# A matrix product with scaled sum on one Trainium2 core: one weight load for two products, a last store behind the joined section, and one load of addends in two pieces

## The chip, the cores and the metric

The kernel runs on one core of one Trainium2 chip. The core has a matrix engine (TensorE, PE in the profile, with its weight loads as PEld), a vector engine (VectorE, DVE), a scalar engine (ScalarE, ACT), a general engine (GpSimd, POOL), and SyncE (SP), which here only waits on semaphores and issues transfers (DMAs) between the chip's memory (HBM) and the core's. The metric is the device time of one execution in microseconds.

## The reference

```
batch, m, k, n = 16, 512, 1024, 768
x: (16, 512, 1024) float32, weight: (1024, 768) float32, scale = 0.1, add_value: (16, 512, 768) float32
return (scale * np.matmul(x, weight) + add_value).astype(np.float32)
```

So 8192 rows of x, each of 1024 values, are multiplied by one 1024 x 768 matrix, scaled, and added to 8192 rows of 768 addends. Inputs read and output written are 87.03 MB together.

## The kernel before, in words

The rows are cut into 64 tiles of 128 rows; tiles go in groups of 8, of which a partition holds 8 neighbouring rows, so that a transfer of 8 tiles moves long pieces. Everything is in one section with semaphores written out by hand (`tile_critical`, L205 to L210). In it each engine has its own program.

**SyncE** (`sync_engine`, L84) walks the list STREAM (L19) in order: ("x", s, n) loads n tiles of x from tile s on, "w" a half of the weights, "a" the addends, "o" stores results. Ahead of each issue it waits for what that transfer needs. Loads of x (L105) wait until the slots of `xs` (16 tiles) were read by the casts (L101, L102). Loads of addends (L115) wait for all loads of addends before them (L109), and from tile 32 on for the store that empties their slots of `ao` (32 tiles, L113, L114); addends of 48-55 therefore wait for the store of 16-23. Stores (L123) wait until the store two before has landed (L121) and until the results are made (L122). As all issues are on one engine, a wait also holds back all that stands behind it in the list. The list ends with loads of x 56-59 and 60-63, addends 56-63, and the stores of 32-39, 40-47, 48-55 and 56-63. Then SyncE waits until the last two stores have landed (L127, L128).

**ScalarE and GpSimd** (`mover`, L130) cast x to bfloat16, 4 tiles (a move) at a time, into one of two buffers `va`; each does 8 of the 16 casts of a move (L143). Each waits for the load of x and for the buffer to be free.

**VectorE** (`vector_engine`, L146) casts the weights at the start (L151). Then, for each pair of tiles, it transposes one pair of x from `va` to `xt` (`turn`, L158, which waits for both casting engines where a move begins) and finishes another pair: `finish` (L163, L167) takes the products from `mm`, scales them, adds the addends in `ao` and leaves the result there. The order is written out by hand in `group` (L171): wait for the addends of the group of 8, then four times finish a pair and turn a pair that lies four tiles further on. The first two turns of a group take the second half of a move whose first half was turned already; the third and fourth turn take the next move. The wait for addends (L172) stands ahead of all of these, the turns too.

**TensorE** (`tensor_engine`, L187) goes over the tiles, in a loop with 4 of them in its body. Ahead of each pair of tiles it waits for the turn and for the finish that frees the products' space (`mm`, 4 tiles). For each of the 8 pieces of 128 values of k it makes two products, of 512 and of 256 columns of the weights (CUT, L198), each a matmul with the piece of x as its stationary operand (L199). Each matmul becomes a weight load and a product, 1024 of each.

Of the kernel before, what the change touches and what calls it, by code (L numbers as in the profile page):

```python
# [7 lines left out]
P = 128  # L8
G = 8
X_SLOTS = 16  # L10
A_SLOTS = 32
CUT = 512
# [13 lines left out]
]  # L26


@with_exitstack
def kernel(  # L30
# [8 lines left out]
    nc = tc.nc  # L39
# [7 lines left out]
    _, N = weight.shape  # L47
    T = M // P
    KC = K // (2 * P)
    KJ = 2 * KC  # L50
# [3 lines left out]
    out_v = out_f.rearrange("(g p t) n -> p g t n", p=P, t=G)  # L54
    w_v = weight.rearrange("(c p r) n -> p c (r n)", p=P, r=2)

    def rows(view, s, n):
        assert s // G == (s + n - 1) // G
        return view[:, s // G, s % G:s % G + n, :]
# [5 lines left out]
    ao = const.tile([P, A_SLOTS, N], fp32, name="ao")  # L65
    w_bf = const.tile([P, KJ, N], bf16, name="w_bf")
    va = [const.tile([P, MOVE * KC, 4, 64], bf16, name=f"va{i}") for i in range(VA_BUFS)]
    xt = const.tile([P, XT_TILES, KC, P], fp32, name="xt")
    mm = psum.tile([P, MM_BUFS, 1024], fp32, name="mm")

    w_sem = [tc.alloc_semaphore(f"w{i}") for i in range(2)]
    x_sem = [tc.alloc_semaphore(f"x{i}") for i in range(X_SLOTS // MOVE)]
    a_sem = tc.alloc_semaphore("a")
    o_sem = [tc.alloc_semaphore(f"o{i}") for i in range(2)]
    by_act, by_pool, pool_go, turned, casts, done, made = (
        tc.alloc_semaphore(name)
# [4 lines left out]
    def slot(t):  # L81
        return (t + G) % A_SLOTS

    def sync_engine(eng):  # L84
        loads, stores, known = [], [], {}

        def need(sem, value):
            if known.get(sem, 0) < value:
                eng.wait_ge(sem, value)  # L89
                known[sem] = value  # L90

        for op, s, n in STREAM:
            last = s + n - 1
            if op == "w":
                dst = ao[:, s:s + n, :].rearrange("p (c r) n -> p c (r n)", r=2)
                move, sem = eng.dma_start(dst, w_v[:, s // 2:(s + n) // 2, :]), w_sem[s // 4]
            elif op == "x":
                k = s % X_SLOTS
                if last >= X_SLOTS:
                    moved = 8 * (last + 1 - X_SLOTS) // MOVE  # L100
                    need(by_act, moved)  # L101
                    need(by_pool, moved)  # L102
                    if n == 2 * MOVE:
                        eng.sem_inc(x_sem[k // MOVE + 1], 16)
                move = eng.dma_start(xs[:, k:k + n, :], rows(x_v, s, n))  # L105
                sem = x_sem[k // MOVE]
            elif op == "a":
                if loads:
                    need(a_sem, 16 * len(loads))  # L109
                if slot(s) == 0:  # L110
                    need(casts, KJ)
                if s >= A_SLOTS:
                    i = stores.index((s - A_SLOTS, n))  # L113
                    need(o_sem[i % 2], 16 * (i // 2 + 1))  # L114
                move = eng.dma_start(ao[:, slot(s):slot(s) + n, :], rows(add_v, s, n))  # L115
                sem = a_sem
                loads.append((s, n))
            else:
                i = len(stores)
                if i > 1:  # L120
                    need(o_sem[i % 2], 16 * (i // 2))  # L121
                need(made, MADE + last + 1)  # L122
                move = eng.dma_start(rows(out_v, s, n), ao[:, slot(s):slot(s) + n, :])  # L123
                sem = o_sem[i % 2]
                stores.append((s, n))
            move.then_inc(sem, 16)
        for i in (len(stores) - 2, len(stores) - 1):  # L127
            need(o_sem[i % 2], 16 * (i // 2 + 1))  # L128

    def mover(eng, copy, parity, count, go=None):  # L130
        if go is None:
            eng.preload_act_table(mybir.ActivationFunctionType.Copy)  # L132
        with eng.Fori(16, 16 * (T // X_SLOTS) + 1, 16) as i:
            for q in range(X_SLOTS // MOVE):
                eng.wait_ge(x_sem[q], i)
                eng.wait_ge(turned, i + (4 * q - 12) if q < 3 else i)  # L136
                if go is not None:
                    eng.sem_inc(go, 1)
                k = MOVE * q
                src = xs[:, k:k + MOVE, :].rearrange("p i (c b k) -> p (i c) b k", b=4, k=64)  # L140
                for a in (parity, parity + 2):
                    for b in range(4):
                        copy(va[q % VA_BUFS][32 * b:32 * b + 32, :, a, :],  # L143
                             src[32 * a:32 * a + 32, :, b, :]).then_inc(count, 1)

    def vector_engine(eng):  # L146
        ao_g = ao.rearrange("p (g t) n -> p g t n", t=G)

        def cast_w(s, n):
            eng.wait_ge(w_sem[s // 4], 16)  # L150
            eng.tensor_copy(w_bf[:, s:s + n, :], ao[:, s:s + n, :]).then_inc(casts, n)  # L151

        def turn(move, half, moves=None):
            if half == 0:
                eng.wait_ge(by_act, moves)
                eng.wait_ge(by_pool, moves)  # L156
            q = 2 * half * KC
            eng.transpose(  # L158
                xt[:, 2 * half:2 * half + 2, :, :].rearrange("p i c m -> p (i c m)"),
                va[move % VA_BUFS][:, q:q + 2 * KC, :, :].bitcast(fp32).rearrange("p c a k -> p (c a k)"),  # L160
            ).then_inc(turned, 2)

        def finish(pair, at, products):  # L163
            eng.wait_ge(done, products)  # L164
            a = ao_g[:, at, 2 * pair:2 * pair + 2, :]
            q = 2 * (pair % 2)
            eng.scalar_tensor_tensor(  # L167
                a, mm[:, q:q + 2, 0:N], float(scale), a,
                op0=mybir.AluOpType.mult, op1=mybir.AluOpType.add).then_inc(made, 2)

        def group(i, at, last):  # L171
            eng.wait_ge(a_sem, i)  # L172
            for p in range(4):
                finish(p, at, i + (4 * p - 12) if p < 3 else i)
                if p < 2 or not last:
                    turn(1 if p < 2 else 0, p % 2, i + 8 if p == 2 else i)

        cast_w(0, 4)
        cast_w(4, 4)
        turn(0, 0, 8)  # L180
        turn(0, 1)
        with eng.Fori(16, 2 * T, 16) as i:
            group(i, bass.ds((i // 16) % (A_SLOTS // G), 1), False)
        s = slot(T - G) // G
        group(2 * T, slice(s, s + 1), True)

    def tensor_engine(eng):  # L187
        eng.sem_inc(turned, TURNED)
        eng.sem_inc(made, MADE)
        eng.wait_ge(casts, KJ)  # L190
        with eng.Fori(TURNED + 2, TURNED + 2 + T, XT_TILES) as i:
            for q in range(XT_TILES):
                if q % 2 == 0:
                    eng.wait_ge(turned, i + q if q else i)
                    eng.wait_ge(made, i + q if q else i)
                for j in range(KJ):
                    x2 = xt[:, q, j // 2, :].bitcast(bf16).rearrange("p (m r) -> p r m", r=2)
                    for n0, n1 in ((0, CUT), (CUT, N)):  # L198
                        m = eng.matmul(  # L199
                            mm[:, q, n0:n1], x2[:, j % 2, :], w_bf[:, j, n0:n1],  # L200
                            start=(j == 0), stop=(j == KJ - 1))
                if q % 2:
                    m.then_inc(done, 4)

    with tc.tile_critical(no_gpsimd_drain=True):  # L205
        sync_engine(nc.sync)
        mover(nc.scalar, nc.scalar.copy, 0, by_act)
        mover(nc.gpsimd, nc.gpsimd.tensor_copy, 1, by_pool, pool_go)
        vector_engine(nc.vector)
        tensor_engine(nc.tensor)  # L210


# [33 lines left out]
```

## Time and profile before

| What | Value |
|---|---|
| Median of 3 runs | 211.11 us (210.85 to 211.26) |
| The profiled execution's own time | 210.75 us |
| Its span, first to last instruction | 208.7 us |
| Bytes moved, mean rate over the span | 87.03 MB, 417 GB/s |
| DMA engines' time in packets, share of the span | 97.7% |
| PE busy | 171.2 us (82%), 1024 matmuls |
| PEld busy | 101.5 us (49%), 1024 weight loads of 99 ns |
| DVE busy | 98.0 us (47%) |
| ACT and POOL busy | 134.7 us (65%) and 135.4 us (65%) |
| Mean granted clock of PE | 0.974 |

The profile is of one execution. A line of instructions gives the start and the length in us, the engine, the line of the kernel, the operation, what it writes and reads with the shape, the number of instructions merged into it, and in brackets how long the engine had been idle and who released it. A table by stretches gives for each stretch of the span the busy time of each engine with its instructions, the granted clock (1.00 is full speed), the share of the DMA engines and GB/s. "Busy tenths" cut the span in 40 slices of 5.2 us, one digit each.

### The profile page before, as it was taken

The page shows a single profiled execution, that of the slowest core. Times are in us where ns is not written, and L with a number is a line of the kernel's source. Part 1 is how long each engine was busy: PE and PEld are TensorE (multiplying, and loading weights), DVE is VectorE, ACT ScalarE, POOL GpSimd, SP SyncE. Part 2 cuts the span into 40 slices and gives each one's busy share as a digit, 9 for nine tenths or more (in the row PEclk, how much of TensorE's full clock was granted, in tenths as well). Part 3 has the DMA queues.
Part 4 walks back from the last instruction along what each step waited for, and adds up shares of the span by engine and source line. Part 5 has one row for each costly group of instructions (what it writes and reads, how often), then busy time and mean ns, then how long its engine had stood idle before and what let it go on. Part 6 is the DMA issues. An engine that isn't in the chain of part 4 may idle for free.

```text
span 208.7 us, 2743 instructions
## 1 busy us (share of the span) xinstructions
PE 171.2 (82%) x1024; PEld 101.5 (49%) x1024; DVE 98.0 (47%) x66; ACT 134.7 (65%) x129; POOL 135.4 (65%) x132
## 2 busy tenths in 40 slices
PE   0000899999999999999999999999996699999600
PEld 0000455566556666666666666655663366665300
DVE  0045325555555555555555555555522825555300
ACT  2392966995499999988780799459960399900000
POOL 0398966996499999999680799559970299900000
PEclk9999999999999999999999999999999799999975
DMA  6999999999999999999999999999999999999785
GB/s 210 419 435 437 433 427 430 446 449 433 402 427 477 399 411 477 396 452 419 415 438 411 454 424 429 452 422 433 419 429 429 424 451 415 443 438 429 339 382 226
DMA packets 4576, 87.03 MB, mean 417 GB/s; under 512 B 480, under 2 KB 480, under 8 KB 992
## 3 DMA queue, kind: packets, MB, share of 16 engines
q1 hardware_dynamic: 4576, 87.03, 97.7%
HBM read 61.87 MB, written 25.17 MB: 417 GB/s over the span
## 4 chain that ended last, share of the span: by engine, by line
DMA 45%; PE 40%; POOL 5%; DVE 3%; issue 1%; SPq 0%; DVEq 0%; POOLq 0%
PE mm L199 40%; DMA out_dram<-ao 27%; DMA ao<-in_add_value_dram 14%; POOL va L143 5%; DMA xs<-in_x_dram 4%; DVE ao L167 2%; DVE xt L158 1%; DVEq L167 0%; SPq L105 0%; SPq L115 0%; DVEq L164 0%; DVEq L156 0%; POOLq L136 0%; SPq L89 0%; SPq L241 0%
## 5 line engine op out<-in xcount | busy, mean ns | idle before, releaser
L199 PE MATMUL mm<-w_bf,xt 128*128 128x512 bf16 (+1 forms) x1024 | 171.2, 331 | 25.4 <-DVE xt L158 25.4
L143 POOL CAST va<-xs 32x1024 bf16<-32x1024 f32 x128 | 135.2, 1056 | 47.2 <-DMA xs<-in_x_dram 31.4
L143 ACT CAST va<-xs 32x1024 bf16<-32x1024 f32 x128 | 133.5, 1043 | 46.7 <-DMA xs<-in_x_dram 40.9
L199 PEld LDWEIGHTS mm<-w_bf,xt 128*128 128x128 bf16 x1024 | 101.5, 99 | 94.8 <-DVE xt L158 25.8
L167 DVE SCALAR_TENSOR_TENSOR ao<-mm,ao 128x1536 f32 (+1 forms) x32 | 56.2, 1757 | 81.1 <-PE mm L199 72.9
L158 DVE STREAM_TRANSPOSE xt<-va 128x1024 f32<-128x1024 f32 x32 | 39.5, 1235 | 5.8 <-POOL va L143 5.7
L151 DVE CAST w_bf<-ao 128x3072 bf16<-128x3072 f32 x2 | 4.5, 2265 | 13.6 <-DMA ao<-in_weight_dram 13.6
L132 ACT ACT_TABLE_LOAD x1 | 1.3, 1283 | 0.9 <-SPq L205 0.9
L227 POOL MEMSET const-float32-0.0<- 128x1 f32 x1 | 0.1, 98 | 0.2 <-issue 0.2
L227 POOL MEMSET const-bfloat16-1.0<- 128x1 bf16 x1 | 0.1, 100 | 0.0
L227 POOL MEMSET const-float32-1.0<- 128x1 f32 x1 | 0.1, 98 | 0.0
L227 POOL MEMSET const-uint8-127<- 128x1 uint8 x1 | 0.1, 98 | 0.0
## 6 DMA issues: line engine op xcount, KB each, us to landing
ao<-in_add_value_dram SPq DMA_DIRECT2D x8, 3072.0 KB, 17.0
out_dram<-ao SPq DMA_DIRECT2D x8, 3072.0 KB, 27.2
xs<-in_x_dram SPq DMA_DIRECT2D x8, 2048.0 KB, 21.3
xs<-in_x_dram SPq DMA_DIRECT2D x4, 4096.0 KB, 23.1
ao<-in_weight_dram SPq DMA_DIRECT2D x2, 1536.0 KB, 12.3
```

The costliest lines, as they stand in the source:

```text
L132: eng.preload_act_table(mybir.ActivationFunctionType.Copy)
L143: copy(va[q % VA_BUFS][32 * b:32 * b + 32, :, a, :], src[32 * a:32 * a + 32, :, b, :]).then_inc(count, 1)
L151: eng.tensor_copy(w_bf[:, s:s + n, :], ao[:, s:s + n, :]).then_inc(casts, n)
L158: eng.transpose(xt[:, 2 * half:2 * half + 2, :, :].rearrange("p i c m -> p (i c m)"), va[move % VA_BUFS][:, q:q + 2 * KC, :, :].bitcast(fp ...
L167: eng.scalar_tensor_tensor(a, mm[:, q:q + 2, 0:N], float(scale), a, op0=mybir.AluOpType.mult, op1=mybir.AluOpType.add).then_inc(made, 2)
L199: m = eng.matmul(mm[:, q, n0:n1], x2[:, j % 2, :], w_bf[:, j, n0:n1], start=(j == 0), stop=(j == KJ - 1))
L227: nc = _bacc.Bacc("TRN2", target_bir_lowering=False, num_devices=1)
```

## The change

It has three parts.

First, the matmul is replaced by `product`: it issues the weight load by itself, once for each piece of x, and then the two products of 512 and 256 columns, marked as bringing no load of their own.

Second, the addends of 48-55 are loaded as 48-51 and 52-55. The second piece reports to a semaphore of its own, `a_late`, which does not take part in the order of the other loads of addends. TensorE raises `a_late` at the start by as much as the first six groups ask for; VectorE waits for it ahead of the third finish of every group but the last.

Third, the store of 56-63 leaves STREAM and is issued after the section in which the engines are synchronised by hand, so that its place and its completion are set by the framework: the section's end joins all engines, and then the store is issued. The waits of SyncE for the last two stores go.

```diff
-    ("x", 44, 4), ("a", 40, 8), ("x", 48, 8), ("o", 16, 8), ("o", 24, 8), ("a", 48, 8),
+    ("x", 44, 4), ("a", 40, 8), ("x", 48, 8), ("o", 16, 8), ("o", 24, 8), ("a", 48, 4), ("a", 52, 4),
     ("x", 56, 4), ("x", 60, 4), ("a", 56, 8), ("o", 32, 8), ("o", 40, 8), ("o", 48, 8),
-    ("o", 56, 8),
 ]
+LAST = (56, 8)
...
-                if loads:
+                if loads and s % G == 0:
                     need(a_sem, 16 * len(loads))
...
-                    i = stores.index((s - A_SLOTS, n))
+                    i = next(j for j, (a, b) in enumerate(stores) if a <= s - A_SLOTS < a + b)
...
-                sem = a_sem
-                loads.append((s, n))
+                if s % G:
+                    sem = a_late
+                else:
+                    sem = a_sem
+                    loads.append((s, n))
...
-        for i in (len(stores) - 2, len(stores) - 1):
-            need(o_sem[i % 2], 16 * (i // 2 + 1))
...
             for p in range(4):
+                if p == 2 and not last:
+                    eng.wait_ge(a_late, i)
                 finish(p, at, i + (4 * p - 12) if p < 3 else i)
...
+    def product(eng, acc, x_j, w_j, j):
+        eng.ldweights(x_j, tile_position=(0, 0))
+        for n0, n1 in ((0, CUT), (CUT, N)):
+            m = eng.add_instruction(mybir.InstMatmult(
+                start_tensor_calc=(j == 0), stop_tensor_calc=(j == KJ - 1),
+                tile_size=(P, P), tile_position=(0, 0), ldweights=False,
+                name=nc.get_next_instruction_name(), engine=eng.engine,
+                ins=[eng.lower_ap(w_j[:, n0:n1]), eng.lower_ap(x_j, for_matmul_weights=True)],
+                outs=[eng.lower_ap(acc[:, n0:n1])]))
+        return m
...
+        eng.sem_inc(a_late, 16 * (T // G - 2))
...
-                    for n0, n1 in ((0, CUT), (CUT, N)):
-                        m = eng.matmul(
-                            mm[:, q, n0:n1], x2[:, j % 2, :], w_bf[:, j, n0:n1],
-                            start=(j == 0), stop=(j == KJ - 1))
+                    m = product(eng, mm[:, q, :], x2[:, j % 2, :], w_bf[:, j, :], j)
...
+    s, n = LAST
+    nc.sync.dma_start(rows(out_v, s, n), ao[:, slot(s):slot(s) + n, :])
```

More of the change, by code (lines that the diff above doesn't have):

```diff
@@ L72 @@
     x_sem = [tc.alloc_semaphore(f"x{i}") for i in range(X_SLOTS // MOVE)]
-    a_sem = tc.alloc_semaphore("a")
+    a_sem, a_late = (tc.alloc_semaphore(n) for n in ("a", "a_late"))
     o_sem = [tc.alloc_semaphore(f"o{i}") for i in range(2)]
```

## The prediction, made before the changed kernel was run

> **What bounds the kernel now.** I read the page's busy tenths first, then the timeline of TensorE (PE), VectorE (DVE) and GpSimd (POOL) around the one dip, then stretches cut at the changes of the granted clock, then the end.
>
> ```profile
> PE   0000899999999999999999999999996699999600
> PEclk9999999999999999999999999999999799999975
> DMA  6999999999999999999999999999999999999785
> ```
>
> The DMA row is full from the second slice to slice 37: 87.03 MB at 417 GB/s over the span, so bytes are the bound and earlier compute there moves no byte. Only the last three slices have DMA room (7, 8, 5), and what decides there is when the last products are ready. PE is busy all along too, except for one dip (6, 6) at 157 to 167 us with a lower clock beside it.
>
> ```profile
> 149.82 9.91 PE L199 MATMUL mm<-w_bf,xt 128*128 128x512 bf16 x60
> 163.59 33.05 PE L199 MATMUL mm<-w_bf,xt 128*128 128x512 bf16 x192 [3.86 <-DVE xt L158]
> ...
> 151.15 1.24 DVE L158 STREAM_TRANSPOSE xt<-va 128x1024 f32<-128x1024 f32 x1
> 160.62 1.76 DVE L167 SCALAR_TENSOR_TENSOR ao<-mm,ao 128x1536 f32 x1 [8.23 <-DMA ao<-in_add_value_dram]
> 162.30 1.24 DVE L158 STREAM_TRANSPOSE xt<-va 128x1024 f32<-128x1024 f32 x1
> ...
> 174.25 1.25 DVE L158 STREAM_TRANSPOSE xt<-va 128x1024 f32<-128x1024 f32 x1 [1.70 <-POOL va L143]
> ...
> 165.42 17.45 POOL L143 CAST va<-xs 32x1024 bf16<-32x1024 f32 x16 [9.94 <-DMA xs<-in_x_dram]
> ```
>
> Here DVE waits 8.23 us for the addends of 48-55, the transposes queued behind that wait are late, and PE stands still for 3.86 us with 192 of 1024 matmuls (tiles 52 to 63) to go. Then the second gate: tiles 56-59 can't be multiplied before POOL has cast their x (it begins when x lands, 165.42) and DVE has turned it (174.25, having waited for POOL).
>
> ```profile
> 160.42:163.83 3.41, 0.24 (x2) 0.12 (x3) 1.00 0.99 423
> 163.83:167.25 3.42, 3.42 (x13) 1.68 (x12) 0.50 1.02 436
> 167.25:170.66 3.41, 3.41 (x22) 2.03 (x21) 1.00 1.07 459
> ...
> 194.55:197.97 3.42, 2.10 (x14) 1.06 (x11) 1.00 0.80 345
> ...
> 20.47:23.89 3.42, 2.34 (x8) 1.03 (x9) 1.00 1.05 453
> ```
>
> The columns are PE busy, weight loads busy, granted clock, DMA share, GB/s. After 3.41 us with 0.24 us of PE work the clock fell to 0.50, and 13 matmuls fit where 22 did; after a full stretch it came back. A stretch with 2.10 us of work (61%) did not lower it; one at the start with 2.34 us (69%) did not yet raise it, since the next stretch is also slow (13 matmuls).
>
> The end, in the same columns with all engines (PE, loads, DVE, ACT, POOL):
>
> ```profile
> 184.00:196.00 12.00, 12.00 (x75) 7.23 (x74) 4.91 (x4) 0.00 (x0) 0.00 (x0) 1.00 1.01 436
> ...
> 197.00:198.00 1.00, 0.00 (x0) 0.00 (x0) 1.00 (x1) 0.00 (x0) 0.00 (x0) 1.00 0.07 25
> 198.00:199.00 1.00, 0.00 (x0) 0.00 (x0) 0.51 (x1) 0.00 (x0) 0.00 (x0) 1.00 0.06 25
> 199.00:200.00 1.00, 0.00 (x0) 0.00 (x0) 0.00 (x0) 0.00 (x0) 0.00 (x0) 1.00 0.92 393
> ```
>
> PE ends at 196.66, DVE's last finish runs from 196.75 to 198.51, the last store is issued at 198.59; the DMA engines have run dry from 197 to 199.4. So the path that sets the end is: x of 56-59 lands, cast, turn, 64 pairs of matmuls, finish, last store (8.7 us to landing), exit.
>
> **Part 1, one weight load for two products.** It drops 512 of 1024 loads of 99 ns. The matmuls remain. DVE's last finishes begin at 181.18, 186.35, 191.55 and 196.75, each released by PE: 5.2 us for two tiles, which is 16 pairs (512 and 256 columns), so 325 ns a pair. In the trace the starts of the matmuls lie alternately 216 ns (after 512 columns) and 109 ns (after 256) apart: twice the columns, twice the time, and what is fixed per matmul is 2 x 109 - 216 = 2 ns. Each of these matmuls has its own load of 98 ns in front, so the loads run beside the products, and nearly nothing of them is in the pace. A load dropped per pair gains at most 2 ns, 0.13 us over the last 64 pairs; the other bound is that the load that is left is no longer done ahead: a loss of 98 ns x 64 = 6.3 us there. Value taken: 0, by the row of 109 ns, in which even the shorter product covers a load; now two products cover one.
> [...]
>
> **Part 2, addends of 48-55 in two loads.** One more issue on SP (0.33 us, row of L115), ahead of the two x issues; the DMA engines have the store of 24-31 before them then, so this costs 0. By the chain, that load was issued at 145.44, when the store of 16-23 had landed, and landed at 160.29: 14.85 us for that store of 24-31 and itself, 3.1 MB each, 7.4 us each. Its first half then lands 3.7 us earlier, at 156.6. DVE needs 3.3 us from landing to PE's restart (160.29 to 163.59): restart at 159.9, where PE ran out at 159.73. So the 3.86 us stall shrinks to 0.2. The second half lands when the whole did, 160.3; its new wait stands ahead of the third finish, which waits for PE until about 165.4 anyway: 0.
> Next late thing: tiles 52-55 are 4 x 2.6 = 10.4 us, now warm, so PE is done at 170.3 (record 170.5). Tile 56 waits for a transpose that still ends at 174.25 + 1.25 = 175.50, since x is behind the same bytes in a full queue, and POOL's cast begins when it lands. PE restarts at 175.55. Before, PE reached tile 56 at 196.66 - 20.8 - 0.16 (the last record outlasts its 109 ns of pace by 0.16) = 175.70. The gain is 0.15 us; **the stall is moved, not removed**: 5.0 us of idle directly ahead of the last 64 pairs.
> Price of that: before, the cold stretch (3.4 us at half clock, 1.7 us lost) was absorbed by the wait for x. Now it is on the path. If the stretches lie as in this profile (next ends at 170.66, 174.07, 177.49, 180.90), 170.66 to 174.07 is empty, the clock falls at 174.07; 174.07 to 177.49 holds 1.94 us of work (57%, below the 69% that did not raise it), so it rises at 180.90: 5.35 us at half clock, **2.68 us lost**. If they lie otherwise: a cold time between 2.4 us (just enough work to raise it at once) and 6.8 us (two stretches), a loss of 1.2 to 3.4 us.
> [...]
>
> **Part 3, last store behind the joined section.** Off the path: the exit's join. Now the last landing is at 207.27, SP's join (L205) runs from 207.48 to 207.79, the closing part (L241) to 208.69: 1.42 us. The store's landing is then followed by the closing part alone, about 0.9: -0.52. On the path: DVE's end to issue was 0.08 us; the join's answers between the engines take 0.31, so about 0.3: +0.22 (bounds 0 and 0.5). Moved past on SP: the two waits for stores 48-55 and 56-63 go, and the wait for 40-47 ahead of the issue, which had landed by 192.5; no other issue is behind it.
>
> **Sum**, against the profiled execution (span 208.7, time 210.75): -0.15 + 2.68 + 0.22 - 0.52 = +2.23 us, 213.0. The runs' median is 211.11, 0.36 above that execution: 213.3. With the middle of the losses from 1.2 to 3.4 us, 2.3, it is 213.0. I take **213.2**, nearer to the first, since its positions were seen.
>
> **Rivals.**
> (a) The gap stays warm. If the 5.0 us of idle is split by a stretch's end so that neither part counts as idle, nothing is lost: -0.15 + 0.22 - 0.52 = -0.45, 210.7 (210.5 to 210.9 by the join's bounds): not slower. It decides where idle fills too little of each stretch: 7% of work lowered the clock, 61% did not, the point is between. If only up to 0.24 us of work lowers it, 5.05 + 0.24 - 3.41 = 1.9 us of the 3.41 us of possible positions do so ahead of the restart and another 0.24 behind it, 62% of them; if up to 2.10 us does, all do. For it: only that. Against it: in this profile's positions an entire stretch is empty. Chance 0.18.
> (b) The split does not do what it says: both halves land together because the queue mixes them. Then the stall and the cold stretch stay where they were, and only part 3 counts: -0.3, 210.8. Against it: the load and the x behind it landed one after the other (160.3, 165.4). Chance 0.06.
> (c) The remaining loads become visible, say because a load can't be done ahead while two products share the weights: up to 98 ns x 512 = 50 us of PE, and with PE's start at 21.5, its 171 us of work and the 12 us from its end to the span's, some 255. Against it: part 1. Chance 0.04.
> The forecast, a cold restart on the path, gets 0.72, with its own range 211.9 (loss 1.2) to 214.1 (loss 3.4).
>
> **Numbers.** A measurement of this kernel tells about 0.2% (0.4 us) from no change. Faster by more: half of (a) and a third of (b), 0.11. Within: the rest of these, 0.13. Slower: forecast and (c), 0.76. The likeliest has less than 8 in 10, so the range takes in (a) and (b): 210.5 to 214.2.
>
> **What would show it.** Right: PE's gap at 159.7 gone or under 0.5 us; a gap of some 5 us that ends at 175.5, released by a transpose that waited for POOL; granted clock 0.50 after it; about 22 to 24 us from there to PE's end; the last store issued at some 201 us; under 1 us from its landing to the span's end; matmuls still 325 ns a pair with 512 loads. Wrong: clock 1.00 after the gap (then (a)); the gap still at 160 (then (b)); a pace above 325 ns (then (c)) or below 323 (then part 1 was undervalued); x of 56-59 landing before 163 us.

## The result, and the profile after

The changed kernel takes 212.65 us (median of 10 runs, 211.70 to 213.01), the kernel before 211.10 us (10 runs, 210.82 to 211.88). The ratio is 1.0066, with a 95% interval of 1.0047 to 1.0084: slower by 1.0 to 1.8 us. The profiled execution took 212.22 us, with a span of 210.2 us where the one before had 208.7.

The page's busy tenths of the changed kernel, the same three rows as of before:

```profile
PE   0000999999999999999999999999998946999700
PEclk9999999999999999999999999999999995999985
DMA  6999999999999999999999999999999999999577
```

The dip of PE has moved by two slices to the right, so it now ends where the last eight tiles begin, and the low clock stands behind it. The dip of the DMA row at the end is deeper (5 instead of 7 in the third slice from the end).

The timelines of PE, DVE and POOL around it (start and length in us; a few matmul records are missing from this trace, so counts and single idle times are a little off):

```profile
148.79 10.24 PE L193 MATMUL mm<-w_bf,xt 128*128 128x512 bf16 x61
159.83 10.57 PE L193 MATMUL mm<-w_bf,xt 128*128 128x512 bf16 x63 [0.81 <-DVE xt L159]
175.47 22.98 PE L193 MATMUL mm<-w_bf,xt 128*128 128x512 bf16 x126 [5.07 <-DVE xt L159]
...
156.86 1.76 DVE L168 SCALAR_TENSOR_TENSOR ao<-mm,ao 128x1536 f32 x1 [5.18 <-DMA ao<-in_add_value_dram]
...
174.17 1.25 DVE L159 STREAM_TRANSPOSE xt<-va 128x1024 f32<-128x1024 f32 x1 [7.06 <-POOL va L144]
...
165.34 17.45 POOL L144 CAST va<-xs 32x1024 bf16<-32x1024 f32 x16 [9.90 <-DMA xs<-in_x_dram]
```

The stall at 160 us has nearly gone: DVE's wait for the addends is 5.18 us instead of 8.23, and PE's idle time 0.81 us by its row instead of 3.86, of which some 0.3 us is a pair of products missing from the trace. But x of 56-59 lands when it did (POOL begins at 165.34, before at 165.42), the transpose comes when it did (174.17, before 174.25), and PE, done with tiles 52-55 at 170.41, stands still for 5.07 us until 175.47. From there to PE's end are 22.98 us; before, the same 64 pairs took 21.0.

Stretches cut at the changes of the clock (PE busy, weight loads, DVE, ACT, POOL, then granted clock, DMA share, GB/s):

```profile
169.34:172.75 3.41, 1.07 (x7) 0.20 (x2) 0.00 (x0) 3.31 (x5) 3.23 (x4) 1.00 1.01 432
172.75:176.17 3.42, 0.70 (x3) 0.26 (x2) 2.00 (x2) 3.35 (x4) 3.24 (x4) 0.50 1.07 460
176.17:179.58 3.41, 3.41 (x12) 0.76 (x5) 2.04 (x2) 3.34 (x4) 3.17 (x5) 0.50 1.00 432
179.58:182.99 3.41, 3.41 (x22) 1.06 (x11) 0.00 (x1) 2.62 (x3) 3.09 (x3) 1.00 0.94 404
```

The stretches are not chosen freely: the granted clock changed at 27.30, 163.83, 167.25 and 201.38 us in the profile before and at 25.98, 172.75, 179.58 and 203.47 us here, and these changes lie whole multiples of 3.41 us apart (before 136.53, 3.41 and 34.13 us, that is 40, 1 and 10 of them; here 146.77, 6.83 and 23.89 us, that is 43, 2 and 7). The half clock in the tables of three experiments below (6.83, 6.83 and 3.42 us) fits this.

The clock falls at 172.75 inside the gap and is back only at 179.58. So PE worked 4.11 us (175.47 to 179.58) at half clock and lost half of it, 2.05 us, right ahead of the end.

The end: first stretches with the same columns, then, from SP's timeline, the last store's issue:

```profile
198.00:199.00 1.00, 0.45 (x4) 0.00 (x0) 0.44 (x1) 0.00 (x0) 0.00 (x0) 1.00 0.06 25
199.00:200.00 1.00, 0.00 (x0) 0.00 (x0) 1.00 (x1) 0.00 (x0) 0.00 (x0) 1.00 0.00 0
200.00:201.00 1.00, 0.00 (x0) 0.00 (x0) 0.32 (x1) 0.00 (x0) 0.00 (x0) 1.00 0.00 0
201.00:202.00 1.00, 0.00 (x0) 0.00 (x0) 0.00 (x0) 0.00 (x0) 0.00 (x0) 1.00 0.92 393
```

```profile
200.60 0.33 SPq L224 DMA_DIRECT2D out_dram<-ao  x1
```

The DMA engines wait until 201 us, before until 199. The store is issued 0.28 us behind DVE's end at 200.32 (before 0.08), lands 8.7 us later at 209.3, and the span ends 0.9 us behind that (before 1.4).

### The profile page after: what moved, and what is told of

Its sections match the earlier page's. It is cut to its first block, busy times and chain, and to the rows that moved or that the text cites. A ratio compares the mean times of both kernels' runs of the same rounds, so it can differ in the third digit from the quotient of the medians.

```text
span 210.2 us, 2215 instructions
## 1 busy us (share of the span) xinstructions
PE 170.3 (81%) x1008; PEld 50.8 (24%) x512; DVE 97.9 (47%) x66; ACT 134.7 (64%) x129; POOL 135.4 (64%) x132
## 4 chain that ended last, share of the span: by engine, by line
DMA 63%; POOL 15%; PE 11%; issue 2%; SPq 2%; DVE 1%; POOLq 0%; DVEq 0%
DMA xs<-in_x_dram 29%; DMA out_dram<-ao 27%; POOL va L144 15%; PE mm L193 11%; DMA ao<-in_add_value_dram 7%; DVE ao L168 1%; SPq L115 1%; DVE xt L159 1%; SPq L105 1%; SPq L96 0%; POOLq L137 0%; SPq L104 0%; POOLq L139 0%; SPq L89 0%; DVEq L157 0%
## 5 line engine op out<-in xcount | busy, mean ns | idle before, releaser
L193 PE MATMUL mm<-w_bf,xt 128*128 128x256 bf16 (+1 forms) x1008 | 170.3, 330 | 28.1 <-DVE xt L159 27.3
L191 PEld LDWEIGHTS <-xt 128*128 128x128 bf16 x512 | 50.8, 99 | 147.2 <-issue 118.3
```

The source lines that it names most:

```text
L191: eng.ldweights(x_j, tile_position=(0, 0))
L193: m = eng.add_instruction(mybir.InstMatmult(start_tensor_calc=(j == 0), stop_tensor_calc=(j == KJ - 1), tile_size=(P, P), tile_position=(0 ...
```

## The experiments

The theory: the split moves PE's stall to the place ahead of the last 64 pairs, where the half clock that follows is on the path. The rivals: the weight loads, the store behind the join, or the split by another way than the clock.

**Part 1 alone** (the kernel before with `product` of the diff, nothing else).

> The kernel before with part 1 alone (512 weight loads instead of 1024). Theory (loads run beside the products): a pair of products stays at 325 ns, the stall of 3.9 us at 160 stays, time as before, 211.1 within 0.2 us. [...]

Measured 211.13 us, ratio 0.9997 (0.9978 to 1.0016). From its table of groups, first the products, then the loads:

```profile
L190 PE MATMUL mm<-w_bf,xt 128*128 128x256 bf16 (+1 forms) x1008 | 170.4, 330 | 26.9 <-DVE xt L158 26.0
...
L188 PEld LDWEIGHTS <-xt 128*128 128x128 bf16 x512 | 50.8, 99 | 146.0 <-issue 118.6 <-DVE xt L158 27.3
```

Half of the loads' 101.5 us is gone and PE's busy time is what it was (171.2 before; 16 records are missing). The loads were beside the products. In this profile the half clock at the old stall lasted 6.8 us, twice as long as in the one of before (PE's timeline, then the stretches):

```profile
163.44 33.90 PE L190 MATMUL mm<-w_bf,xt 128*128 128x512 bf16 x189 [4.50 <-DVE xt L158]
...
158.37:161.79 3.42, 0.57 (x4) 0.07 (x1) 1.32 (x1) 0.00 (x0) 0.00 (x0) 1.00 1.03 438
161.79:165.20 3.41, 1.76 (x6) 0.48 (x4) 3.41 (x4) 0.08 (x1) 0.00 (x0) 0.50 1.00 428
165.20:168.62 3.42, 3.42 (x13) 0.83 (x6) 0.97 (x1) 3.35 (x4) 3.19 (x4) 0.50 1.06 453
```

PE ended at 197.34 here instead of 196.65, with the same program for everything else. The weight loads are not the reason: the profile of part 3 alone (below), with all 1024 loads, has 6.8 us of half clock at the old stall too, and PE ends at 197.12 (33.60 us from its restart, 33.05 in the profile before). So where the stretches fall is a matter of the execution, and a longer time at half clock delays PE's end even at the old place.

**Part 2 alone.**

```diff
-    ("x", 44, 4), ("a", 40, 8), ("x", 48, 8), ("o", 16, 8), ("o", 24, 8), ("a", 48, 8),
+    ("x", 44, 4), ("a", 40, 8), ("x", 48, 8), ("o", 16, 8), ("o", 24, 8), ("a", 48, 4), ("a", 52, 4),
```

with `a_late` as in the diff, and parts 1 and 3 undone.

> The kernel before with part 2 alone (addends of 48-55 in two loads). Theory (the stall moves from 160 to 170-175 and the clock falls ahead of the last 64 pairs): 0.2 us gained at the restart and 1.2 to 3.4 us lost at half clock, 2.0 as in the changed kernel's profile, so 212.1 to 214.1, some 212.9. Rival (the loss of the changed kernel comes from the store behind the join): 210.9 to 211.1.

Measured 213.04 us, ratio 1.0087 (1.0061 to 1.0113). The whole loss comes with this part. PE's timeline in its profile has the same gap, and the stretches by clock show two slow ones behind it:

```profile
159.95 10.58 PE L205 MATMUL mm<-w_bf,xt 128*128 128x512 bf16 x63 [1.08 <-DVE xt L161]
175.61 23.78 PE L205 MATMUL mm<-w_bf,xt 128*128 128x512 bf16 x126 [5.09 <-DVE xt L161]
```

```profile
171.11:174.52 3.41, 0.00 (x0) 0.00 (x0) 0.21 (x1) 3.34 (x4) 3.23 (x4) 1.00 1.01 432
174.52:177.94 3.42, 2.33 (x8) 1.05 (x9) 3.42 (x3) 3.35 (x4) 3.24 (x4) 0.50 1.07 460
177.94:181.35 3.41, 3.41 (x13) 1.67 (x12) 0.41 (x1) 3.31 (x5) 3.23 (x4) 0.50 0.97 418
```

From 175.61 to 181.35 are 5.74 us at half clock, 2.87 lost; the 64 pairs took 23.78 us.

**Part 3 alone** (last store behind the section, its waits gone, the rest as before).

> The kernel before with part 3 alone (last store behind the joined section). Theory: issue 0.2 us later behind DVE's end, exit 0.55 us shorter behind the landing, together -0.3, 210.8. Rival (the join costs what the changed kernel lost): 212 or more.

Measured 210.72 us, ratio 0.9987 (0.9968 to 1.0006). The join does not cost what the change lost; that it gains is likely by this and not shown, since the interval reaches past 1.

**The changed kernel with the gap filled.** Its tile loop is cut ahead of tile 56, and between the two loops stands (FILL is 44, late is the count that tile 56 waits for)

```diff
+        eng.wait_ge(made, late)
+        x_j = w_bf[:, 0, 0:P]
+        for k in range(FILL):
+            if k == 0:
+                eng.ldweights(x_j, tile_position=(0, 0))
+            eng.add_instruction(mybir.InstMatmult(
+                start_tensor_calc=True, stop_tensor_calc=True,
...
+                ins=[eng.lower_ap(w_bf[:, 0, 0:256]), eng.lower_ap(x_j, for_matmul_weights=True)],
+                outs=[eng.lower_ap(mm[:, 0, N:N + 256])]))
```

> The changed kernel with 44 matmuls of 256 columns added in PE's gap ahead of tile 56 (109 ns each, 4.8 us of 5.1), which write to columns of the products' space that nothing reads; the output is as before. Theory (the clock fell because of the gap): granted clock 1.00 up to PE's end at 196.3, time 0.4 us under the kernel before, 210.7. Rival (the split delays the end by something other than the clock, such as the order on DVE): 212.2 to 213 as the changed kernel.

Measured 210.12 us (210.03 to 210.47), ratio 0.9957 (0.9942 to 0.9972). PE's timeline, then stretches over the gap and behind it:

```profile
170.17 4.97 PE L227 MATMUL mm<-w_bf 128*128 128x256 bf16 x44
175.65 20.75 PE L194 MATMUL mm<-w_bf,xt 128*128 128x256 bf16 x124 [0.51 <-DVE xt L160]
```

```profile
170.41:175.65 5.24, 4.73 (x45) 0.10 (x1) 1.53 (x2) 5.12 (x6) 4.94 (x6) 1.00 0.95 408
175.65:179.06 3.41, 3.41 (x22) 1.07 (x11) 2.50 (x2) 3.31 (x5) 3.23 (x4) 1.00 0.99 425
```

PE waits for the same transpose and starts at the same time (the second row begins with a product of 256 columns, so the record of the 512 columns ahead of it, 0.2 us, is missing), the clock stays at 1.00, the 64 pairs take 21.0 us with that record (20.75 without it), and useless work has made the kernel 2.5 us faster than the changed one. With the clock kept up, nothing of the loss is left. It is also 1.0 us faster than the kernel before, not 0.4 as expected. The sum of the other terms (restart, issue, exit) is about -0.5 us, and the executions of the kernel before with the highest granted clock (0.973 to 0.975) took 210.5 to 211.0, so the remaining 0.5 us fits a kernel before that loses time to the clock in many of its executions too.

**Half of that filling** (22 matmuls instead of 44).

> As e4_warm with 22 added matmuls instead of 44: 2.4 us of work at the start of PE's gap, so that some 2.7 us of idle is left, less than one 3.41 us stretch. Theory (a stretch with little enough work lowers the clock, it need not be empty: in the changed kernel's profile one with 1.07 us of work, 31%, did): a stretch over the idle holds at least 0.7 us of work, 21%, so by position some runs fall to half clock and some do not, single runs spread between 210.1 and 213, median 210.5 to 212. Rival (only an empty stretch lowers the clock): always 1.00, 210.1 as e4_warm.

Measured 210.42 us (median, a little under the range expected), ratio 0.9971 (0.9947 to 0.9995). Of 12 executions 8 took 210.12 to 210.56 us and 4 took 211.80 to 212.12. Only one was profiled, and it is of the latter (PE's timeline, then the stretches):

```profile
175.68 22.66 PE L194 MATMUL mm<-w_bf,xt 128*128 128x512 bf16 x128 [2.68 <-DVE xt L160]
```

```profile
173.38:176.79 3.41, 1.11 (x7) 0.39 (x4) 2.42 (x2) 3.34 (x4) 3.23 (x4) 1.00 0.94 404
176.79:180.21 3.42, 3.42 (x13) 0.79 (x6) 1.62 (x2) 3.35 (x4) 3.24 (x4) 0.50 1.00 431
```

A gap of 2.68 us is shorter than a stretch and still lowered the clock, after a stretch with 1.11 us of work (33%). The rival, that only an empty stretch does so, falls.

**x of 56-59 between the two halves of the addends** (the changed kernel, and in the list)

```diff
-    ("x", 44, 4), ("a", 40, 8), ("x", 48, 8), ("o", 16, 8), ("o", 24, 8), ("a", 48, 4), ("a", 52, 4),
-    ("x", 56, 4), ("x", 60, 4), ("a", 56, 8), ("o", 32, 8), ("o", 40, 8), ("o", 48, 8),
+    ("x", 44, 4), ("a", 40, 8), ("x", 48, 8), ("o", 16, 8), ("o", 24, 8), ("a", 48, 4), ("x", 56, 4),
+    ("a", 52, 4), ("x", 60, 4), ("a", 56, 8), ("o", 32, 8), ("o", 40, 8), ("o", 48, 8),
```

> The changed kernel with the load of x 56-59 put between the two halves of the addends of 48-55 in the list. Theory: x 56-59 lands at some 161.5 instead of 165.1, its cast and turn end near 172, PE's gap shrinks from 5.1 to some 1.3 us, the clock stays at 1.00, PE ends 4 us earlier than in e4_warm, near 192.7. The last store is then issued near 195, while the DMA engines still work. Gain over e4_warm, if all 16 DMA queues are dry from 197.4 to 199.4 there: 2 us, 208.1. Rival (one of the queues is behind, as the last landing of the store of 48-55 came 1.3 to 1.6 us behind the 15 others in both profiles, and sets the end however early the store is issued): 0.4 to 0.8 us, 209.3 to 209.7. If the stretch of idle still lowers the clock: 1 to 2 us slower than either.

Measured 209.96 us (209.65 to 210.07), ratio 0.9927 (0.9905 to 0.9949): the fastest kernel of this study. Timelines of PE and SP, then two stretches at the end:

```profile
172.02 20.98 PE L193 MATMUL mm<-w_bf,xt 128*128 128x512 bf16 x128 [1.39 <-DVE xt L159]
...
195.14 0.33 SPq L224 DMA_DIRECT2D out_dram<-ao  x1
```

```profile
198.00:199.00 1.00, 0.00 (x0) 0.00 (x0) 0.00 (x0) 0.00 (x0) 0.00 (x0) 0.50 0.91 393
...
205.60:206.60 1.00, 0.00 (x0) 0.00 (x0) 0.00 (x0) 0.00 (x0) 0.00 (x0) 0.50 0.06 25
```

PE's gap is 1.39 us, PE ends at 192.99, and the last store is issued 5.5 us earlier than in the changed kernel, while the queues work: there is no dry time at 198. Yet this gains little over the filled gap: 0.16 us by the medians, 0.14 by the last landings of the two profiles (207.21 and 207.07). The two kernels were measured on different chips, on which the kernel before took 211.10 and 211.32 us, so the medians say no more than some tenths; the ratios to it, 0.9957 and 0.9927, would say 0.6 us. The last line shows what holds the end: from 205.6 to 206.6 us the DMA share is 0.06, one engine of sixteen. In this store 15 parts landed by 205.59 and one at 207.07, as the store of 48-55 did at 198.35 and 199.81. From the one store to the next are 7.24 us for the 15 parts and 7.26 us for the late one, so the late one had no pause either, and issuing the store earlier could not help it. That it is the same engine both times is inferred from this; the trace doesn't tell which engine a part is of. The rival for the end is right: all of the 2 us was not to be had. Its price of 0.4 to 0.8 us is above what the medians and the landings show, and not excluded by the ratios.

**The last kernel without part 1, and without part 3.**

> As e6_x_between with part 1 undone (1024 weight loads again). No clock loss blurs this one. Theory (loads run beside the products): same as e6_x_between, 209.95 within 0.2 us, PE's last 64 pairs still 21.0 us. [...]

Measured 210.10 us (209.94 to 210.22). PE's last 64 pairs took 20.98 us again, with 1024 loads:

```profile
172.00 20.98 PE L203 MATMUL mm<-w_bf,xt 128*128 128x512 bf16 x126 [1.40 <-DVE xt L159]
```

By this row the loads cost nothing here either. The time is within the 0.2 us expected of 209.96, but says little, since it is of a third chip, on which the kernel before took 210.71 us instead of 211.32.

> As e6_x_between with part 3 undone (last store in the list again, waits for the last two stores at the end). The store is issued while the queues work, so its issue is off the path. Theory: only the exit differs, 1.4 instead of 0.9 us behind the last landing, 0.5 us slower than e6_x_between, 210.5. Rival (the framework's exit costs the same either way): 209.95.

Measured 210.23 us (210.13 to 210.45), beside the 210.10 of the kernel without part 1 on the same chip, and the 209.96 on another. In the profiles the span ends 1.4 us behind the last landing here, and 0.9 us in the kernel with part 3, as expected; in the time only 0.13 of that 0.5 is seen on the same chip (0.27 against the other). The profiled execution of this kernel was the slowest of its 12. The last landing was some 0.15 us earlier here (206.93 beside 207.07 and 207.14). Whether that belongs to the change or to the late part is open.

## Why the prediction was right, and where it was off

What is right is the mechanism, shown by the rows above and by the filled gap. That the time lies in the range says less: 210.5 to 214.2 us would have taken in rivals (a) and (b) as well.

- **Part 1 at nothing**: right. A pair takes 325 ns with 512 loads (four finishes of the profile after start 5.2 us apart), and neither adding it alone nor undoing it in the last kernel changed PE's pace.
- **The stall is moved, not removed**: right. Expected: restart of tile 52 at 159.9, PE idle from 170.3 to 175.55. Measured: 159.83, 170.41 to 175.47.
- **The cold restart on the path**: right in kind. The term was mis-sized: 2.68 us came from the old profile's positions; this profile had 2.05, that of the split alone 2.87. The positions were not the same again (the clock first rose at 27.30 us before, at 25.98 after, at 24.33 with the split alone, with 22, 22 and 23 matmuls in the stretch behind that, and 13 in the stretch ahead of it before and after; the first matmul came at 21.4 to 21.6 in all three), so a draw between 1.2 and 3.4 us is the better picture, and both lie in it.
- **The step that did not hold**: "before, the cold stretch (3.4 us at half clock, 1.7 us lost) was absorbed by the wait for x". That was so in the one execution that was profiled. The wait absorbs about that much and no more. In the profiles of part 1 alone and of part 3 alone the time at half clock at the old place was 6.8 us, and PE ended 0.7 and 0.5 us later. The runs of the kernel before order by their mean granted clock: of the 29 beside the first four experiments, those at 0.973 to 0.975 took 210.5 to 211.0 us, those at 0.967 to 0.968 took 211.1 to 211.5 (one 211.9), those at 0.960 to 0.961 took 211.7 to 211.8. Later runs of it on other chips follow this with exceptions (211.2 and 211.3 us at 0.972, 211.1 at 0.974), and the mean clock also counts the half clock behind PE's end, so this is a sign and no proof. By it the 0.36 us between its profiled execution and its median, which I added as a constant, was most likely itself the price of the clock at the old stall, which the changed kernel no longer has. Without it the sum is 212.6 (loss 2.3) to 213.0 (loss 2.68), against a measured 212.65; with it the forecast of +2.1 us was too large against a measured +1.55.
- **Part 3**: +0.22 on the path, measured 0.28 - 0.08 = 0.20; -0.52 at the exit, measured 0.9 instead of 1.4. With the terms as measured, the sum is -0.23 (restart) + 2.05 + 0.20 - 0.5 = +1.5 us, which is the difference of the spans (210.2 - 208.7). The forecast for this pair of executions was +2.23, and nearly all of what it had too much is the cold term (2.68 instead of 2.05).
- **Rival (a)**, a gap that stays warm: no execution of the changed kernel was near 210.1, where the filled gap put it. Stretches with 31% and 33% work lowered the clock, so the point at which (a) decides lies above that. An estimate in the prediction's way from 1.11 us of work: 5.07 + 2 x 1.11 - 3.41 = 3.88 us of positions, more than the 3.41 there are, so a gap of 5.07 us leaves (a) none.
- **Rivals (b) and (c)** did not come: the gap at 160 went (0.81 us by its row), and the pace stayed (325 ns a pair).
- Missed: the DMA share of 0.06 ahead of the last store. I read it as engines run dry; 15 of 16 were, and one part was late by 1.3 to 1.6 us. With PE done at 192.99 (x between the halves), the late part set the end: 207.07 us, 1.48 behind the 15 others.

## What to carry to other kernels

When an earlier load removes a stall, ask what the freed engine waits for next, and where that new wait stands: here the stall that ended just ahead of the last piece of work cost its cold clock in full (2.05 and 2.87 us in two profiles), while the same stall earlier was partly absorbed (part 1 alone: 6.8 us of half clock, PE's end 0.7 us later). Here, with the DMA engines in packets for 97.0% of the span, splitting a load did not bring the bytes behind it noticeably earlier (POOL's cast of x 56-59 began at 165.34 us instead of 165.42). The list that also puts x ahead of the second half of the addends was 1.3% faster than the change as made (209.96 against 212.65 us, not measured side by side; the ratios to the kernel before, 0.9927 and 1.0066, say 1.4%). Before you count weight loads as a cost, look whether the spacing of the products follows their columns (here 216 ns behind 512 columns and 109 ns behind 256, with loads of 98 ns).

## What was not expected of the hardware

- The clock fell after stretches of 3.41 us with 31% and 33% of PE work (1.07 and 1.11 us), not only after empty ones; one with 61% did not lower it. It rose again after full stretches and, at the start of the split alone, after one with 86% (2.94 us); stretches with 20%, 68% and 69% (0.70, 2.33 and 2.34 us) did not raise it. That is why a restart in the middle of a stretch cost 4.11 and 5.74 us at half clock here and not 3.41 at most. A gap of 2.68 us lowered it in the profiled execution and, by their times alone, in 3 of the other 11; the gap of 1.39 us in the fastest kernel did not in the profiled one.
- One of the 16 parts in which a store landed fell behind: the last part of a store landed 0.5 us behind the next to last at 145 us, 1.1 us at 185 and 1.6 us at 199.9 in the profile before, and 1.3 us at 199.7 in the one after. Why is not known; it was not tried. With the gap filled a second part came late (the store of 48-55: 14 parts by 198.17 us, then 199.35 and 199.65; the DMA share from 197 to 199 us is 0.12, two engines of sixteen); what held that one up is not shown.
